# Output projection that ends with block 7, and a fixed order for the first tile pair of the MLP's up stage

## The chip, the cores and the metric

The kernel runs on one core of a Trainium2 chip. The metric is the device time of one execution in microseconds (us). Three runs of the kernel before gave 2959.98, 2953.46 and 2958.82 us; the median is 2958.82.

A core has five engines that each take their own instructions in order: PE (TensorE, matrix products; PEld is its weight load), DVE (VectorE), ACT (ScalarE), POOL (GpSimd) and SP (SyncE, which issues the DMAs here). They meet only through semaphores. PE writes PSUM, a small memory of eight banks of 128 x 512 float32; DVE and ACT read it from there. Everything else lies in SBUF.

## The reference

The reference is one streaming step of a two-layer network: layer 0 is a gated linear recurrence, layer 1 is differential attention, and each is followed by an output projection and a squared-ReLU MLP. Cut to what the change touches:

```
m = o @ w_o                                   # output projection, 1024 -> 1024
h = h + rmsnorm(m, norm_g[l, 1])
a = rmsnorm(h, norm_g[l, 2])
f = square(relu(a @ w_up)) @ w_down           # 1024 -> 4096 -> 1024
h = h + rmsnorm(f, norm_g[l, 3])
```

There are 1024 prompt rows and 128 sample rows; the kernel treats them as nine blocks of 128 rows, 0 to 7 for the prompt and 8 for the sample. All is float32.

## The kernel before

**Products.** A float32 operand is split into a high part (cast to the multiplier's format, on ACT) and a low part (the difference, on DVE). A product is then three matmuls: high x high, high x low, low x high.

**Output projection** (`out_proj`, lines 624 to 668). For each block, 48 matmuls (L281 to L283) into the tile `pm`; then the block's chain: a sum of squares on ACT (L216 on `pm`), a few tiny operations for the reciprocal root (L203 to L211), `t<-pm` on DVE (L655), `hb<-hb,t` (L658), a second sum of squares (L216 on `hb`), the tiny operations again, and `t<-hb` (L275), the normed row block. Halves of 512 columns of `t` are transposed on PE (`half_T`, four transposes into one bank: L242), and from PSUM ACT writes the high part (L246) and DVE the low part (L247) into the big operand tiles `aTh` and `aTl`. Blocks go in the order 0 to 8 in layer 0, and 0 4 1 5 2 6 3 7 8 in layer 1 (`LATE`), where one column half of blocks 0 to 3 was projected earlier (`EARLY`), so that 24 matmuls are left for each of these.

**Up stage** (`mlp_up`). The prompt part of `a @ w_up` is done by a seven-product scheme (Strassen-Winograd) on 2 x 2 quarters: rows of blocks 0 to 3 against rows of blocks 4 to 7, columns 0:512 against 512:1024. A11 and A12 are the two column halves of blocks 0 to 3, A22 the second half of blocks 4 to 7; S1 to S4 are sums of quarters. `pair_sums(blk, j)` forms them for blocks j and j+4 in place (L678 to L681, four operations of 128 x 512, on DVE or POOL). S2 goes to the aT tiles; S1, S3 and S4 are transposed by `s_ops` into the tiles a1, a3, a4 (high `h`, low `l`), one `half_T` per j, through two PSUM banks `T` (L235 for the transposes).

The 4096 columns are taken as 16 pairs of tiles. Per pair there are seven products P1 to P7 of 12 matmuls (L238, 128 x 512), and `smp`, the sample block against the same weights (24 matmuls of 128 x 256 into bank U). P1 and P2 use A11 and A12; P4 A22; P5 S1; P6 S2; P7 S3; P3 S4. The raw weights of a pair and their sums (`sums`, L735 to L738, on DVE for the first pair, then on POOL) are split as s0, s1, s2 in turn (L720 ACT, L721 DVE): s0 raw and s1 sums for the first pair, s2 raw and s0 sums for the second. Results are added up on DVE: c11 = P1 + P2 (L797), u2 = P6 + p1 (L823), c22 = P7 on top of P6, + p1 + P5 (L832, L833), c12 = P3 on top of P5, + u2 (L850), c21 = P4 on top of P7 and P6, + p1 (L865). PSUM bank tags are X, U, Y (two), Z (two), T (two).

The first pair goes in the order `P1 P2 T S1 P6 S3 P5 S4 P7 smp P3 P4`, where T is the split of s1. The two transposes of the sample block and the split of the second pair's weights stand with S4 and P7. `keep` holds the tiles `t`; the area of s2 is laid over it after S4.

**What sets the order.** The tile layer keeps each engine's list in an order that its own time model finds, under the data's dependencies; PE's up-stage matmuls are pinned in program order (`pin`, L228). ACT and DVE are not pinned.

Of the kernel before, what the change touches and what calls it, by code (L numbers as in the profile page):

```python
# [2 lines left out]

# [16 lines left out]
P = 128  # L20
D = 1024
# [34 lines left out]
SAMPLE = ['yk0 yl1 yn0', 'ys0', 'xf0', 'xk1 xn1 yv0', 'ys1', 'xf1', 'xl2 yv1', '']  # L56

EARLY = {1: (0,), 2: (1,), 6: (2,), 7: (3,)}
LATE = (0, 4, 1, 5, 2, 6, 3, 7, 8)
PAIR = 2  # L60


def view(ap, off, dims):
# [4 lines left out]
def tile_kernel(ctx, tc, x_prompt, x_sample, cache_k, cache_v, state_hgrn, norm_g, w_hgrn_in,  # L68
# [539 lines left out]
    def out_proj(w, gains, gain, o_src, osc, g_post, h_old, h_new, g_pre, order, W=None, early={}):  # L608
# [3 lines left out]
        with ExitStack() as os_:  # L612
# [9 lines left out]
                if b not in early:  # L622
                    prepare(block(b), b, o_src, osc, gain, pp, ts)

            order = LATE if early else range(NB)
            todo = [b for b in order if b not in early]
            for b in todo[:3]:
                prep(b)
# [4 lines left out]
            for b in order:  # L633
                pm = ps_wide("pm")
                halves = [early[b]] if early.get(b) is not None else []
                for nh in range(len(halves), 2):
                    halves.append(pm[:, nh * 512:(nh + 1) * 512])
                    out_half(halves[nh], W, nh, b)
                if todo:
                    prep(todo.pop(0))  # L640
                t = block(b) if b in early else blk[b]
                if early.get(b) is not None:
                    ss = ts.tile([P, 2], F32, name="ss", bufs=3)
                    for nh in range(2):
# [12 lines left out]
                nc.sync.dma_start(out=hb, in_=h_old(b))  # L657
                (nc.gpsimd if b in POOL_OUT else nc.vector).tensor_tensor(out=hb, in0=hb, in1=t, op=ALU.add)  # L658
                nc.sync.dma_start(out=h_new[b * P:(b + 1) * P, :], in_=hb)
                pre_norm(hb, g2, t, t, ts, b)  # L660
                done.add(b)
                if b == NBP:
                    continue
                if b < NP:
                    half_T(t[:, 0:512], aTh[:, b, 0:4], aTl[:, b, 0:4])
                half_T(t[:, 512:D], aTh[:, b, 4:8], aTl[:, b, 4:8])
                if b < NBP and b ^ NP in done:
                    pair_sums(blk, b % NP, nc.vector if len(done) > NBP - 3 else nc.gpsimd)
        return blk, keep

    def pair_sums(blk, j, eng):

        e, o = blk[j], blk[j + NP]
        a11, a12, a21, a22 = e[:, 0:512], e[:, 512:D], o[:, 0:512], o[:, 512:D]
# [2 lines left out]
        tt(out=a21, in0=a11, in1=a21, op=ALU.subtract)  # L679
        tt(out=a11, in0=a22, in1=a11, op=ALU.subtract)  # L680
        tt(out=a12, in0=a12, in1=a11, op=ALU.subtract)  # L681
        half_T(a11, aTh[:, j + NP, 0:4], aTl[:, j + NP, 0:4])

    def again(*a, **k):

# [2 lines left out]
    def mlp_up(l, blk, keep):  # L688
        wu = w_up[l].rearrange("(k p) n -> p k n", p=P)
        with ExitStack() as ms, ExitStack() as ls:  # L690
            R = Area(ms, "ur", "wst s0h s0l s1h s1l a4h a1h a1l a3h a3l a4l p1 u2 c0 hs", side="right")
            B = Area(ms, "ub", "X U Y:2 Z:2 T:2", space=PSUM)
            L = []
            SA = {}
            mk = {"A11": (0, 0), "A12": (0, 4), "S2": (NP, 0), "A22": (NP, 4)}
# [19 lines left out]
            def split(st, n, parts):

# [63 lines left out]
            for i in range(NFP):  # L780
                sets = (raw, tset)
                C = {}
                seq = "P1 P2 T S1 P6 S3 P5 S4 P7 smp P3 P4" if i == 0 else "P1 P6 P2 P5 P7 smp P3 P4"
                for op in seq.split():
                    if op == "P1":
                        X = bank("X")
# [5 lines left out]
                    elif op == "P2":  # L792
                        c = C["c11"] = cell()
                        if i == 0:
                            V = bank("Z")
                            prod(V, op, sets, True)
                            add(out=c, in0=V, in1=p1, op=ALU.add)  # L797
                            nc.scalar.activation(c, c, AF.Relu)
                        else:
                            prod(X, op, sets, False)  # L800
                            nc.scalar.activation(c, X, AF.Relu)
                        nc.gpsimd.tensor_tensor(out=c, in0=c, in1=c, op=ALU.mult)
                        store(c, "A11", i)
                    elif op == "T":
                        tset = split(st, 1, [(r1, ca), (r0, ca)])
                        sets = (raw, tset)
                        nx = load(1)
                    elif op == "S1":
                        s_ops(op, lambda j: blk[j + NP][:, 512:D])
                    elif op == "S3":  # L810
                        s_ops(op, lambda j: blk[j + NP][:, 0:512])
                    elif op == "S4":
                        s_ops(op, lambda j: blk[j][:, 512:D])
                        for z in range(2):
                            half_T(blk[NBP][:, z * 512:(z + 1) * 512], aTh[:, NBP, 4 * z:4 * z + 4],
                                   aTl[:, NBP, 4 * z:4 * z + 4], transpose, lambda n: bank("T"))
                        keep.close()
                        L.append(Area(ls, "ul", "s2h s2l c:7 hT"))
                    elif op == "P6":
                        Y = bank("Y")  # L820
                        prod(Y, op, sets, True)
# [6 lines left out]
                        prod(Z, op, sets, True)  # L828
                    elif op == "P7":
                        prod(Y, op, sets, False)  # L830
                        c = C["c22"] = cell()
                        add(out=c, in0=Y, in1=p1, op=ALU.add)  # L832
                        add(out=c, in0=c, in1=Z, op=ALU.add)  # L833
                        relu2(c)
                        store(c, "A22", i)
                        if nx is not None:
                            raw = split(nx, 2 * i + 2, [(r0, ca), (r1, ca)])
                            sums(nx, nc.gpsimd)
                    elif op == "smp":
# [7 lines left out]
                    elif op == "P3":  # L847
# [14 lines left out]
                    elif op == "P4":  # L862
# [695 lines left out]
```

## Time and profile before

| | us |
|---|---|
| runs | 2959.98, 2953.46, 2958.82 (median 2958.82) |
| profiled execution, its own time | 2951.5 |
| its span, first to last instruction | 2949.6 |
| PE busy in the span | 2856.6 (97%) |
| DVE / ACT / POOL busy | 1855.0 / 1205.4 / 669.3 |
| mean granted PE clock | 0.991 of full |
| layer 0: last block's projection ends, up stage begins | at 756.6 |
| layer 1: the same | at 2195.2 |

The span is measured from the first instruction to the last; the execution's own time is 1.9 us longer, and 7.3 us below the median of the three runs. "Busy" is the share in which an engine had an instruction under way. A timeline row has start, duration, engine, line, operation, output and inputs, shape and count; in brackets stands the idle time of that engine before it and what ended it. A row with x2 has two instructions merged.

### The profile page before, as it was taken

Reading aid. Unit: us, or ns where it says so; the run is one execution under the profiler, and the core shown is the slowest. Engines: PE = TensorE matmul, PEld = TensorE weight load, DVE = VectorE, ACT = ScalarE, POOL = GpSimd, SP = SyncE. Lnnn points to the kernel's source line nnn. Section 1 sums busy time; section 2 is a strip of 40 time slices with the busy share of each in tenths; the row PEclk is TensorE's granted clock in tenths of the full one; section 3 lists DMA queues with packets and bytes.
Section 4 is the critical chain, followed back from the end, with each engine's and each line's share of the span. In section 5 each row is a group of like instructions: output and inputs, shape, how many; then the busy total and the mean of one; then the engine's idle time right before and its main releaser. Section 6 shows DMA issues by size and latency. Waiting matters only on the chain. (4 is left out here: it accounts for less than half of the span.)

```text
span 2949.6 us, 45368 instructions
## 1 busy us (share of the span) xinstructions
PE 2856.6 (97%) x16897; PEld 2498.0 (85%) x16897; DVE 1855.0 (63%) x3523; ACT 1205.4 (41%) x2597; POOL 669.3 (23%) x558
## 2 busy tenths in 40 slices
PE   7999999989899999999989999998999999999998
PEld 6999999978688887888779999997877888878886
DVE  7777777776644445465875665656685444545567
ACT  5322222343333334443554554556543333434433
POOL 1111111101145442121211110111114454402311
PEclk9999999989999999999999999999999999999999
DMA  4111111142243348587752121313332433577966
GB/s 137 55 53 53 53 53 53 53 149 86 67 140 127 130 152 289 192 282 257 273 167 69 56 78 48 91 45 96 120 107 93 152 129 127 205 258 236 322 198 244
DMA packets 337120, 405.27 MB, mean 137 GB/s; under 512 B 21081, under 2 KB 210690, under 8 KB 336898
## 3 DMA queue, kind: packets, MB, share of 16 engines
q1 hardware_dynamic: 336898, 402.37, 41.3%
q8 instruction: 133, 2.18, 0.3%
q14 instruction: 89, 0.73, 0.1%
HBM read 280.12 MB, written 122.16 MB: 136 GB/s over the span
## 5 line engine op out<-in xcount | busy, mean ns | idle before, releaser
L238 PE MATMUL D<-wh,aTh 128*128 128x512 f32 x896 | 354.7, 396 | 2.8 <-DVE aO L1044 2.8
L238 PE MATMUL D<-wl,aTh 128*128 128x512 f32 x896 | 354.1, 395 | 0.5 <-DVE wl L905 0.5
L238 PE MATMUL D<-wh,aTl 128*128 128x512 f32 x896 | 354.2, 395 | 0.0
L905 DVE TENSOR_TENSOR aTl<-hst,aTh 128x1024 fp32r<-128x1024 f32 x112 | 156.2, 1399 | 186.2 <-ACT aTh L904 177.8
L238 PE MATMUL pj<-whi,aTh 128*128 128x256 f32 x864 | 254.2, 294 | 0.3
L238 PE MATMUL pj<-wlo,aTh 128*128 128x256 f32 x864 | 244.0, 282 | 2.3 <-DVE wlo L182 2.3
L238 PE MATMUL pj<-whi,aTl 128*128 128x256 f32 x864 | 244.1, 283 | 0.0
L904 ACT CAST aTh<-hst 128x1024 fp32r<-128x1024 f32 x112 | 116.7, 1048 | 247.8 <-PE D L238 217.3
L238 PEld LDWEIGHTS D<-wh,aTh 128*128 128x128 f32 x896 | 169.0, 189 | 43.7 <-issue 2.3
L238 PEld LDWEIGHTS D<-wl,aTh 128*128 128x128 f32 x896 | 169.1, 189 | 40.0 <-DVE wl L905 1.0
L238 PEld LDWEIGHTS D<-wh,aTl 128*128 128x128 f32 x896 | 169.1, 189 | 39.4
L238 PEld LDWEIGHTS pj<-whi,aTh 128*128 128x128 f32 x864 | 164.2, 190 | 6.6 <-issue 4.5
L281 PE MATMUL pi<-whi,aTh 128*128 128x256 f32 x576 | 167.1, 290 | 0.7 <-DVE qk L418 0.7
L238 PEld LDWEIGHTS pj<-wlo,aTh 128*128 128x128 f32 x864 | 163.9, 190 | 3.2 <-DVE wlo L182 2.5
L282 PE MATMUL pi<-wlo,aTh 128*128 128x256 f32 x576 | 166.5, 289 | 0.0
L283 PE MATMUL pi<-whi,aTl 128*128 128x256 f32 x576 | 166.3, 289 | 0.0
L238 PEld LDWEIGHTS pj<-whi,aTl 128*128 128x128 f32 x864 | 163.6, 189 | 0.0
L905 DVE TENSOR_TENSOR wl<-wsta,wh 128x1024 fp32r<-128x1024 f32 x112 | 138.9, 1244 | 22.7 <-ACT wh L904 21.2
L756 POOL TENSOR_TENSOR c<-c 128x512 f32<-128x512 f32 x96 | 115.0, 1198 | 166.0 <-ACT c L755 165.4
L755 ACT ACTIVATE c<-c 128x512 f32<-128x512 f32 x96 | 60.7, 632 | 223.1 <-DVE c L833 184.7
L904 ACT CAST wh<-wsta 128x1024 fp32r<-128x1024 f32 x112 | 117.1, 1049 | 77.9 <-PE D L238 28.3
L506 DVE COPY_PREDICATED A<-masks,lv 128x64 f32<-128x64 uint8 x448 | 85.7, 261 | 48.3 <-PE lv L503 44.3
(484 smaller groups left out, 7946.6 us busy)
## 6 DMA issues: line engine op xcount, KB each, us to landing
u_dr<-c SPq DMA_DIRECT2D x224, 256.0 KB, 4.3
hst<-u_dr SPq DMA_DIRECT2D x112, 512.0 KB, 5.4
wsta<-in_w_down_dram SPq DMA_DIRECT2D x96, 512.0 KB, 4.7
wst<-in_w_up_dram SPq DMA_DIRECT2D x32, 1024.0 KB, 6.1
wstb<-in_w_down_dram SPq DMA_DIRECT2D x32, 512.0 KB, 5.1
wstb<-t_dr SPq DMA_DIRECT2D x32, 512.0 KB, 5.3
h_dr<-hb SPq DMA_DIRECT2D x27, 512.0 KB, 2.6
hb<-h_dr SPq DMA_DIRECT2D x27, 512.0 KB, 4.6
```

Source lines behind the costliest of these rows:

```text
L238: pin(nc.tensor.matmul(*a, **k))
L281: matmul(out, lh, rh, start=first, stop=False)
L282: matmul(out, lh, rl, start=False, stop=False)
L283: matmul(out, ll, rh, start=False, stop=last)
L506: nc.vector.copy_predicated(out=view(A[:], o, [(per, 64 // m), (1, m)]), mask=masks[:, li, :].rearrange("p (j i) -> p j i", i=m), data=lv[ ...
L755: nc.scalar.activation(c, c, AF.Relu)
L756: nc.gpsimd.tensor_tensor(out=c, in0=c, in1=c, op=ALU.mult)
L904: nc.scalar.copy(h, st)
L905: vt(out=lo, in0=st, in1=h.bitcast(F32), op=ALU.subtract)
```

## The change

The block orders become 0 1 2 3 4 5 8 6 7 in layer 0 and 0 4 1 5 2 6 8 3 7 in layer 1. The last block (7) leaves the projection without being transposed; step A of the up stage does that, and its `pair_sums`. The first pair of the up stage follows a written list of steps, and inside it the PE, ACT and DVE instructions of the pair are chained in program order. The operands of S1 to S4 are made block by block between products; the sample's product comes after P1 and P2; P4 comes next and gets a bank of its own (Q, added to c21 by one more DVE operation); the second pair's weight split and sums (K) follow the last S4; c22, P3 and c21 end the pair. The order in which PSUM banks are laid out depends on the layer.

```
-LATE = (0, 4, 1, 5, 2, 6, 3, 7, 8)
+LATE = (0, 4, 1, 5, 2, 6, 8, 3, 7)
+FIRST_PAIR = "T P1 S1:01 P2 S1:2 N smp S3:0 A P4 S2:3 S1:3 C11 P6 S3:12 P5 S3:3 S4:0 P7 S4:123 K C22 P3 C21"
...
+    @contextmanager
+    def in_order():
+        traced = nc.cur_bb.bb.instructions
+        have = {id(i) for i in traced}
+        yield
+        for i in list(traced):
+            if id(i) not in have and i.engine in (mybir.EngineType.PE, mybir.EngineType.Activation,
+                                                  mybir.EngineType.DVE):
+                if i.engine in order_of:
+                    tc.add_manual_dep(i, order_of[i.engine].name, ..., reason="order")
+                order_of[i.engine] = i
...
-            order = LATE if early else range(NB)
+            order = LATE if early else (*range(6), NBP, 6, 7)
...
-                if b == NBP:
+                if b == NBP or len(done) == NB:
                     continue
...
-                    pair_sums(blk, b % NP, nc.vector if len(done) > NBP - 3 else nc.gpsimd)
+                    pair_sums(blk, b % NP, nc.vector if len(done) > NBP - 1 else nc.gpsimd)
...
-        half_T(a11, aTh[:, j + NP, 0:4], aTl[:, j + NP, 0:4])
+        if j < NP - 1:
+            half_T(a11, aTh[:, j + NP, 0:4], aTl[:, j + NP, 0:4])
...
-            B = Area(ms, "ub", "X U Y:2 Z:2 T:2", space=PSUM)
+            order = "X T_0 Y_0 Y_1 Z_0 T_1 Z_1 U" if l == 0 else "X T_0 Y_0 Y_1 Z_1 U Z_0 T_1"
+            B = Area(ms, "ub", order + " Y:2 Z:2 T:2", space=PSUM)
...
+            srcs = {"S1": (NP, 512), "S2": (0, 0), "S3": (NP, 0), "S4": (0, 512)}
+            def s_op(name, j):
+                n, (o, k) = name[1], srcs[name]
+                c = slice(j * P, (j + 1) * P)
+                if name == "S2":
+                    h, lo = aTh[:, NP + j, 0:4], aTl[:, NP + j, 0:4]
+                else:
...
+                    h, lo = [x[:, :, c] for x in SA[name]]
+                half_T(blk[o + j][:, k:k + 512], h, lo, transpose, lambda n: bank("T"))
...
-                seq = "P1 P2 T S1 P6 S3 P5 S4 P7 smp P3 P4" if i == 0 else "P1 P6 P2 P5 P7 smp P3 P4"
+                first = ExitStack()
+                if i == 0:
+                    first.enter_context(in_order())
+                seq = FIRST_PAIR if i == 0 else "P1 P6 P2 P5 P7 smp P3 P4"
...
+                    elif op[0] == "S":
+                        for j in op[3:]:
+                            s_op(op[:2], int(j))
+                    elif op == "A":
+                        b = NBP - 1
+                        half_T(blk[b][:, 512:D], aTh[:, b, 4:8], aTl[:, b, 4:8], transpose, lambda n: bank("T"))
+                        pair_sums(blk, b % NP, nc.vector)
+                    elif op == "N":
                         for z in range(2):
                             half_T(blk[NBP][:, z * 512:(z + 1) * 512], aTh[:, NBP, 4 * z:4 * z + 4],
                                    aTl[:, NBP, 4 * z:4 * z + 4], transpose, lambda n: bank("T"))
+                    elif op == "K":
                         keep.close()
                         L.append(Area(ls, "ul", "s2h s2l c:7 hT"))
+                        raw = split(nx, 2, [(r0, ca), (r1, ca)])
+                        sums(nx, nc.gpsimd)
+                    elif op == "P4" and i == 0:
+                        Q = bank("Y")
+                        prod(Q, op, sets, True)
...
+                    elif op == "C21":
+                        c = C["c21"] = cell()
+                        add(out=c, in0=Y, in1=p1, op=ALU.add)
+                        add(out=c, in0=c, in1=Q, op=ALU.add)
+                        relu2(c)
```

Lines move by about 19 to 50: a matmul of the up stage is L238 before and L257 now, a `half_T` evacuation L246/L247 before and L265/L266 now, the pair sums L678 to L681 are now L698 to L701, `t<-hb` L275 is now L294, the weight split L720/L721 is L749/L750.

VectorE, layer 0, the end of the first pair, before (s2 is the second pair's raw weights, s0 its sums; L832, L833 add up c22, L850 c12, L865 c21):

```order
L247 TENSOR_TENSOR a4l<-T,a4h 128x4x128 x2
L721 TENSOR_TENSOR s2l<-wst,s2h 128x1024 x2
L247 TENSOR_TENSOR a4l<-T,a4h 128x4x128 x2
L247 TENSOR_TENSOR aTl<-T,aTh 128x512 x2
L832 TENSOR_TENSOR c<-Y,p_8948 128x512
L833 TENSOR_TENSOR c<-c,Z 128x512
L850 TENSOR_TENSOR c<-Z,u_9019 128x512
L721 TENSOR_TENSOR s0l<-wst,s0h 128x1024 x2
L865 TENSOR_TENSOR c<-Y,p_8948 128x512
```

VectorE at the same place now (L877, L878 add up c22, L895 c12, L914, L915 c21):

```order
L266 TENSOR_TENSOR a4l<-T,a4h 128x4x128 x4
L750 TENSOR_TENSOR s2l<-wst,s2h 128x1024 x2
L877 TENSOR_TENSOR c<-Y,p_8938 128x512
L878 TENSOR_TENSOR c<-c,Z 128x512
L895 TENSOR_TENSOR c<-Z,u_9083 128x512
L750 TENSOR_TENSOR s0l<-wst,s0h 128x1024 x2
L914 TENSOR_TENSOR c<-Y,p_8938 128x512
L915 TENSOR_TENSOR c<-c,Y 128x512
```

The split of s2 stood between the second and the third a4; it now stands behind the fourth, directly ahead of the c22 additions.

VectorE, layer 0, where the last block's chain meets the first S1 operands, before:

```order
L203 TENSOR_SCALAR rs_v<-ss 128x1
L205 RECIPROCAL rs_y<-rs_y 128x1
L207 SCALAR_TENSOR_TENSOR rs_t<-rs_y,rs_v 128x1
L211 SCALAR_TENSOR_TENSOR rs_y<-rs_t,rs_y 128x1
L275 SCALAR_TENSOR_TENSOR t<-hb,rs_y,gb 128x1024
L797 TENSOR_TENSOR c_8950<-Z,p_8948 128x512
L247 TENSOR_TENSOR a1l<-T,a1h 128x4x128 x4
```

and now:

```order
L226 SCALAR_TENSOR_TENSOR rs_t<-rs_y,rs_v 128x1
L266 TENSOR_TENSOR aTl<-pt,aTh 128x512
L230 SCALAR_TENSOR_TENSOR rs_y<-rs_t,rs_y 128x1
L294 SCALAR_TENSOR_TENSOR t<-hb,rs_y,gb 128x1024
L266 TENSOR_TENSOR a1l<-T,a1h 128x4x128 x3
L266 TENSOR_TENSOR aTl<-T,aTh 128x512 x2
L266 TENSOR_TENSOR a3l<-T,a3h 128x4x128
```

The last block (8 before, 7 now) is normed directly ahead of the first a1 in both; c11 (L797) has moved behind the fourth a1.

PE, layer 1, the start of the up stage, before (`pm` is the last block's projection, X the bank of P1, `pt` the bank of a half_T in the projection):

```order
L281 MATMUL pm<-whi,aTh 128x512
L282 MATMUL pm<-wlo,aTh 128x512
L283 MATMUL pm<-whi,aTl 128x512
L238 MATMUL X<-aTh,s0h 128x512
L242 MATMUL pt<-ident,t 128x128 x4
L238 MATMUL X<-aTl,s0h 128x512
```

and now:

```order
L300 MATMUL pm<-whi,aTh 128x512
L301 MATMUL pm<-wlo,aTh 128x512
L302 MATMUL pm<-whi,aTl 128x512
L261 MATMUL pt<-ident,t 128x128 x8
L257 MATMUL X<-aTh,s0h 128x512
L257 MATMUL X<-aTl,s0h 128x512
```

The eight transposes ahead of X are the two halves of block 3, which is now the last but one; P1 reads the first of them and P2 the second.

## Rows read from the trace of the kernel before

**Rows 1.** Busy time of the engines in four stretches of the up stages (--windows).
Columns: stretch, its length, busy us and instructions of each engine, granted PE clock, DMA share, GB/s.

```profile
756.20:808.10 51.90, 39.50 (x194) 32.33 (x193) 33.17 (x51) 21.36 (x36) 11.34 (x10) 0.87 0.15 47
808.10:830.50 22.40, 22.40 (x111) 18.80 (x110) 10.67 (x13) 7.60 (x11) 11.08 (x10) 1.00 0.40 135
2195.20:2241.30 46.10, 37.30 (x192) 29.71 (x191) 31.48 (x49) 21.16 (x36) 11.16 (x9) 0.93 0.17 53
2241.30:2263.70 22.40, 22.40 (x111) 18.79 (x110) 10.67 (x13) 7.64 (x11) 11.09 (x10) 1.00 0.39 135
```

**Rows 2.** Waits of PE, layer 0, 640 to 860 us: total, times, longest.

```profile
PE pt L242 <- DVE t L680: 5.8, 1, 5.8
PE T L235 <- DVE a4l L247: 4.2, 2, 3.2
```

**Rows 3.** Waits of PE, layer 1, 2095 to 2310 us.

```profile
PE pt L242 <- DVE t L680: 4.7, 1, 4.7
```

**Rows 4.** Two idle stretches of PE, each with the stretch behind it (--windows).

```profile
760.40:766.20 5.80, 0.01 (x1) 0.03 (x1) 5.80 (x12) 1.73 (x3) 0.00 (x0) 0.89 0.00 0
766.20:771.40 5.20, 5.20 (x15) 4.22 (x16) 4.15 (x9) 1.94 (x4) 0.00 (x0) 0.50 0.90 299
787.50:790.80 3.30, 0.10 (x2) 0.06 (x1) 3.13 (x4) 1.39 (x3) 1.83 (x1) 0.70 0.00 0
790.80:795.50 4.70, 4.70 (x16) 4.02 (x16) 1.80 (x3) 1.17 (x2) 4.38 (x5) 0.50 0.00 0
```

**Rows 5.** Timeline of PE, layer 0.

```profile
756.58 0.40 PE L238 MATMUL X<-aTh,s0h 128*128 128x512 f32 x1
...
772.02 1.03 PE L235 MATMUL T<-ident,t 128*128 128x128 f32 x8
...
808.09 0.40 PE L238 MATMUL Y<-aTh,s0h 128*128 128x512 f32 x1
```

**Rows 6.** Timeline of PE, layer 1.

```profile
2195.21 0.39 PE L238 MATMUL X<-aTh,s0h 128*128 128x512 f32 x1
...
2241.28 0.40 PE L238 MATMUL Y<-aTh,s0h 128*128 128x512 f32 x1
```

**Rows 7.** Timeline of DVE, layer 0.

```profile
747.49 1.28 DVE L655 SCALAR_TENSOR_TENSOR t<-pm,rs_y,gb 128x1024 f32<-128x1024 f32 x1
748.81 1.23 DVE L658 TENSOR_TENSOR hb<-hb,t 128x1024 f32<-128x1024 f32 x1
...
773.27 0.69 DVE L247 TENSOR_TENSOR a1l<-T,a1h 128x512 fp32r<-128x512 f32 x1
...
787.66 2.36 DVE L721 TENSOR_TENSOR s2l<-wst,s2h 128x1024 fp32r<-128x1024 f32 x2 [0.81 <-ACT s2h L720]
...
797.01 0.69 DVE L832 TENSOR_TENSOR c<-Y,p 128x512 f32<-128x512 f32 x1 [2.95 <-PE Y L238]
797.74 0.69 DVE L833 TENSOR_TENSOR c<-c,Z 128x512 f32<-128x512 f32 x1
```

**Rows 8.** Timeline of ACT, layer 0.

```profile
745.20 1.02 ACT L216 ACTIVATE t<-pm 128x1024 f32<-128x1024 f32 x1 [2.39 <-issue]
...
772.65 0.58 ACT L246 CAST a1h<-T 128x512 fp32r<-128x512 f32 x1 [2.00 <-PE T L235]
...
785.91 2.01 ACT L720 CAST s2h<-wst 128x1024 fp32r<-128x1024 f32 x2
```

**Rows 9.** Timeline of POOL, layer 0: the second pair's weight sums.

```profile
788.97 2.18 POOL L735 TENSOR_TENSOR wst<-wst 128x512 f32<-128x512 f32 x1 [13.97 <-DVE s2l L721]
791.23 1.27 POOL L736 TENSOR_TENSOR wst<-wst 128x512 f32<-128x512 f32 x1
```

**Rows 10.** DMA issues, from the page: size, us from issue to landing.

```profile
h_dr<-hb SPq DMA_DIRECT2D x27, 512.0 KB, 2.6
```

**Rows 11.** Timeline of DVE, layer 1: one tiny operation at three times.

```profile
2147.59 0.89 DVE L207 SCALAR_TENSOR_TENSOR rs_t<-rs_y,rs_v 128x1 f32<-128x1 f32 x1
...
2148.59 1.26 DVE L207 SCALAR_TENSOR_TENSOR rs_t<-rs_y,rs_v 128x1 f32<-128x1 f32 x1
...
2208.38 0.22 DVE L207 SCALAR_TENSOR_TENSOR rs_t<-rs_y,rs_v 128x1 f32<-128x1 f32 x1
```

More of the change, by code (lines that the diff above doesn't have):

```diff
@@ L1 @@
 import math
-from contextlib import ExitStack
+from contextlib import ExitStack, contextmanager
 import concourse.bass as bass
@@ L195, in tile_kernel @@
     rsx = {}
+    order_of = {}
+    @contextmanager
[7 more added lines that the diff above has]
+                if i.engine in order_of:
+                    tc.add_manual_dep(i, order_of[i.engine].name,
+                                      mybir.DependencyInfo(mybir.DependencyClass.NoSync,
+                                                           mybir.DependencyReason.DATA), reason="order")
+                order_of[i.engine] = i
     def rstd_of(ss, n, inv_d, pool, y=None):
@@ L704, in a_op @@
                 return SA[name][0][:, k, :], SA[name][1][:, k, :]
-            def s_ops(name, src):
-                n = name[1]
-                SA[name] = h, lo = (R.tile([P, 4, HT], F32R, name=f"a{n}h", bufs=1),
+            srcs = {"S1": (NP, 512), "S2": (0, 0), "S3": (NP, 0), "S4": (0, 512)}
[5 more added lines that the diff above has]
+                else:
+                    if name not in SA:
+                        SA[name] = (R.tile([P, 4, HT], F32R, name=f"a{n}h", bufs=1),
                                     R.tile([P, 4, HT], F32R, name=f"a{n}l", bufs=1))
-                for j in range(NP):
-                    c = slice(j * P, (j + 1) * P)
-                    half_T(src(j), h[:, :, c], lo[:, :, c], transpose, lambda n: bank("T"))
+                    h, lo = [x[:, :, c] for x in SA[name]]
+                half_T(blk[o + j][:, k:k + 512], h, lo, transpose, lambda n: bank("T"))
             def split(st, n, parts):
@@ L796, in mlp_up @@
                             prod(V, op, sets, True)
[L797 to L801, printed above, removed]
+                            continue
+                        prod(X, op, sets, False)
+                        nc.scalar.activation(c, X, AF.Relu)
+                        nc.gpsimd.tensor_tensor(out=c, in0=c, in1=c, op=ALU.mult)
+                        store(c, "A11", i)
+                    elif op == "C11":
+                        c = C["c11"]
+                        add(out=c, in0=V, in1=p1, op=ALU.add)
+                        nc.scalar.activation(c, c, AF.Relu)
                         nc.gpsimd.tensor_tensor(out=c, in0=c, in1=c, op=ALU.mult)
@@ L807, in mlp_up @@
                         nx = load(1)
[L808 to L813, printed above, removed]
+                    elif op[0] == "S":
[6 more added lines that the diff above has]
+                    elif op == "N":
                         for z in range(2):
@@ L830, in mlp_up @@
                         prod(Y, op, sets, False)
+                    if op == "C22" or op == "P7" and i > 0:
                         c = C["c22"] = cell()
@@ L835, in mlp_up @@
                         store(c, "A22", i)
-                        if nx is not None:
+                        if nx is not None and i > 0:
                             raw = split(nx, 2 * i + 2, [(r0, ca), (r1, ca)])
                             sums(nx, nc.gpsimd)
-                    elif op == "smp":
+                    if op == "smp":
                         U = bank("U")
@@ L861, in mlp_up @@
                             tset = split(nx, 2 * i + 3, [(r1, ca), (r0, ca)])
-                    elif op == "P4":
+                    elif op == "P4" and i > 0:
                         prod(Y, op, sets, False)
@@ L866, in mlp_up @@
                         relu2(c)
+                    elif op == "C21":
[3 more added lines that the diff above has]
+                        relu2(c)
+                first.close()
                 pend = C
```

## Prediction

> **What bounds the kernel now.** I read first the busy times by stretch, then PE's waits, then the timelines around them. The first pair of each layer lasts 51.90 and 46.10 us with PE busy for 39.50 and 37.30; the pair behind it lasts 22.40 and PE is busy for all of it [rows 1]. So PE bounds the up stage from the second pair on, and whatever delays that pair's first dependent product, P6 (808.09 and 2241.28) [rows 5, 6], goes one to one to the end. In the first pair PE idles for 12.4 us (51.90 - 39.50) and 8.8 us. The waits that the trace names are `pt<-ident,t` on the pair sum of the last two blocks (5.8 and 4.7) and the T banks on a4l (4.2) [rows 2, 3]. The idle time is followed by work at 0.50 of full clock, that is 1.2 of 2.4 GHz: 5.2 us of it behind 5.8 us of idle, 4.7 us behind 3.3 [rows 4]. Half clock over 4.7 us costs some 2.35. A pair of 22.40 us is eight equal pieces (seven products and `smp`), 2.8 us each.
>
> The work to be done is nearly the same after: the same products and transposes, one more addition of 0.7 us on DVE per pair, and 0.7 us more on PE nowhere. What can change is only when the operands are ready. So I walked each engine's new list with the durations of before, 0.1 us for a handoff, and wrote down when PE waits.
>
> **Layer 0, the start.** X (P1) starts at about 756.2 instead of 756.58 [rows 5], since one half_T fewer stands ahead, and ends at 759.0; P2 ends at 762.9. The pair sums of blocks 2 and 6 are one chain with the last block's normalisation on DVE, and S1:2's transposes get their operand at about 764.7: 1.8 us idle. The 5.8 us wait of [rows 2] is gone here. But S1 takes only two T banks at first, and the next transpose waits until a1l(0) has read its bank. On DVE a1l(0) stands directly behind the last block's `t<-hb` (the second order listing), because a1 lies over `hb`; it also needs the store of `h_dr` to have landed (2.6 us [rows 10]). That `t<-hb` comes at 770.0 to 771.2, as the last chain goes at the same pace as before, so a1l(0) (0.69 [rows 7], behind a1h, 0.58 [rows 8]) ends at 771.9. PE idles 6.8 us and resumes at the moment at which S1's transposes started before (772.02 [rows 5]). Thus the pieces put ahead (P1, P2) were ahead before too, the wait has only another name, and `smp` (2.8 us), which used to fill a later gap, now stands behind this stall. Half clock follows for about 5 us as in [rows 4]; `smp` ends at 778.8.
>
> **Layer 0, the end of the first pair.** From there P4, P6, P5 and P7 (11.2 us) with six half_Ts of 0.52 (3.1; x8 is two of them in 1.03 [rows 5]) and 3.3 us of small waits for operands one half_T late bring P7's end to 796.4, S4's last transposes at 798.7. P3 is next, and it adds onto the Z bank that holds P5, so it waits until c22's second addition (L878) has read Z. In the first order listing that addition stands behind both s2l. The chain: a4h 0.58, the first s2h 1.0 (half of 2.01) [rows 8], two s2l 2.36, and two additions of 0.7 [rows 7] is 5.3, and with handoffs 5.65: P3 starts at 804.3. Before, L833 ran at 797.74, nine us behind the split of s2 (787.66) [rows 7], and `smp` covered it; here nothing covers it. What is queued behind it on DVE: c12, the split of s0, c21. Half clock then makes P3 5.1 us long (to 809.4). The second pair's P1 uses X and needs only s2 and runs to 812.4. Its P6 takes the bank of Q, which c21's second addition (L915) frees, and it needs s0, whose POOL sums start only once s2l is made (801.7) and take 6.4 by [rows 9] (2.18, 1.27, and two more of 1.27, with gaps) plus a square of 1.0 between: 809.2. Behind c12 (810.2) come its relu and hT on ACT (1.0), s0h (1.0), s0l (2.36) and two additions (1.4): 816.1. PE idles 3.7 us. That is 8.0 later than 808.09. 3.7 us of idle is nearest to the 3.3 of [rows 4], so I add 2.2 for half clock: **+10.2**.
>
> **Layer 1, the start.** Block 3 is now last but one, with only block 7's projection (48 matmuls, 4 x 2.8 = 11.2 us, ending at 2194.9) beside its chain, and X reads block 3. A chain's first half takes 4.84 us unimpeded, from its sum of squares at 745.20 to `hb` at 750.04 [rows 7, 8], and its second half the same 2.29 and 1.28 again: 8.4 us, so it would fit; but three s0h casts stand ahead of its second reciprocal root on ACT, four s0l (2.6 us) ahead of its `hb` on DVE, then the four weight sums (2.7). Walked so, `t<-hb` of block 3 ends at 2198.95, the eight transposes (third listing) wait for it 4.1 us, and aTl comes behind two s1l and block 7's `t<-pm`, at 2203.1. X starts effectively at 2202.9 instead of 2195.21 [rows 6], at half clock, and ends at 2207.85. P2 follows to 2211.4 (2209.5 before), and `smp` ends at 2216.75; here block 7's chain no longer stalls PE, so the 4.7 us of [rows 3] is absorbed in the earlier wait. From the end of `smp` everything goes as in layer 0, 37.3 us to P6: 2254.05, against 2241.28: 12.8 later, and 2.2 for the clock: **+15.0**.
>
> **The sum.** 10.2 + 15.0 = 25.2 on an execution of 2951.5: 2976.7. This execution lies 7.3 below the median, so 2984 on the median; I take 2980, between the two.
>
> **Terms not seen before.** (1) GpSimd beside DVE. Pair sums of blocks 2 and 6 in layer 1 go to POOL now, in the time of block 3's chain. While POOL did pair sums earlier, a tiny DVE operation took 0.89 and 1.26 instead of 0.22 [rows 11]: 1.7 us in all were lost over some 5.4 us of POOL's work. Of this about 1 is slack: +0.7 by the rows, at least 0; I leave it out of the sum. At most all 5.4 are lost, +4.4; this end is the rival (d) below. (2) The new bank order and the Q addition cost PE nothing: 0.7 us on DVE is in the chain above. (3) Half clock behind the 5.65 and 3.7 us: from 0 to 2.6 us each; I take the value nearest in [rows 4].
>
> Of (1) the Trainium skill, in "SBUF — State Buffer", section "SBUF: two separate sides", says that the port pair that GpSimd and VectorE share is an exclusive lock, held for a whole instruction, and that the other engine fully blocks. The two long rows agree in kind, yet DVE lost only 1.7 of 5.4 us; by the rule the sum would be nearer to +29 than to +25.
>
> **Rivals.**
> (a) The clock stays full behind the short stalls at P3 and P6. For it: the first stretch of [rows 1] has a mean clock of 0.87, so half clock is the smaller part of it; against it: both idle stretches of over 3 us in [rows 4] are followed by 0.50. P3 then ends at 807.15 and P6 comes at 814.0, +5.9 in layer 0 and +10.7 in layer 1: +16.6, 2968 to 2975.
> (b) The other side: c22's second addition is done before S4's last transposes end, because ACT and DVE run ahead of PE. For it: ACT is busy for only 21.36 of 51.90 us and DVE for 33.17 [rows 1]; against it: s2l stands behind the fourth a4l in DVE's list and cannot overtake it. From s2l done by 798.7, that is 5.65 us earlier, it decides: no stall at P3, none at P6 (s0 comes 5.6 earlier too), no half clock, 13.8 less per layer: 25.2 - 27.6 = -2.4, 2949 to 2956. It doesn't reach faster by 0.2%, save with a third of the starting stalls gone as well.
> (c) The last blocks' chains go at the unimpeded 8.4 us in both layers: layer 0's 6.8 us stall shrinks to about 1 and X in layer 1 isn't held. That leaves the two ends of the pair, and about +6.5: 2958 to 2966. Against it: before, with the same neighbours, the chain wasn't unimpeded.
> (d) DVE is blocked for the whole of POOL's pair sums, and the stores of `h_dr` land later than 2.6 us, so that a1l waits longer: +28 to +33, 2980 to 2992.
>
> **How the numbers follow.** Forecast 50%, with a range of its own of 2973 to 2987; (a) 20%, (d) 13%, (c) 8%, (b) 7%, and 2% for a gain that I don't see. About 0.2%, 5.9 us, is what a measurement can tell from no change. (b) lies within it or a little beyond, and most of (c) within it too: faster 0.06, same 0.10, slower 0.84. The range of 2960 to 2993 leaves out (b) and most that is beyond it on either side.
>
> **What would show it.** Right: in layer 0 a wait of T's transposes on a1l of about 7 us ending near 772; in both layers a wait of P3 (Z) on the c22 addition of 5 to 6 us, and of the second pair's P6 (Y) on c21 of 3 to 4, with 0.50 clock behind; P6 near 816 and, less layer 0's shift, near 2254; in layer 1 the transposes of `t` ahead of X wait 4 us; the pairs behind at 22.40. Wrong: P3 that follows S4's transposes without a wait (the end-of-pair terms fall, 8 us and more per layer), a first PE resumption in layer 0 well before 770, or X in layer 1 near 2196.

## The result, and the profile after

Four runs of the changed kernel gave 2980.68, 2981.65, 2983.99 and 2983.99 us: median 2982.82, against 2957.39 for the kernel before (four runs). The ratio is 1.0084 with a 95% interval of 1.0068 to 1.0100: slower by 25.4 us. The profiled execution spans 2979.0 us, 29.4 more than before.

Where the time went is seen first in three anchors: the first matmul of layer 0's down stage (into the bank D), the first matmul of its last group, and the first matmul of layer 1's down stage. Timeline of PE, before and then after:

```profile
1144.02 0.40 PE L238 MATMUL D<-wh,aTh 128*128 128x512 f32 x1
1494.76 0.47 PE L238 MATMUL D<-wh,aTh 128*128 128x512 f32 x1
2576.97 0.40 PE L238 MATMUL D<-wh,aTh 128*128 128x512 f32 x1
```

```profile
1157.05 0.40 PE L257 MATMUL D<-wh,aTh 128*128 128x512 f32 x1
1507.69 0.48 PE L257 MATMUL D<-wh,aTh 128*128 128x512 f32 x1
2607.39 0.40 PE L257 MATMUL D<-wh,aTh 128*128 128x512 f32 x1
```

Up to the down stage layer 0 lost 13.0 us; in that down stage nothing changed (350.74 and 350.64); from the second anchor to the third, with layer 1's attention, projection and up stage, 17.5 us were lost (1082.21 became 1099.70). With the 0.1 gained between them that makes 30.4; the last stretch gave 1.0 back.

The first pair and the second one of each layer, which answer to [rows 1] (stretch, length, busy us of PE, PEld, DVE, ACT, POOL, granted clock, DMA share, GB/s):

```profile
756.34:819.54 63.20, 40.16 (x196) 31.73 (x194) 35.93 (x55) 21.81 (x38) 9.97 (x9) 0.86 0.13 41
819.54:841.94 22.40, 22.40 (x103) 18.72 (x104) 11.07 (x13) 6.93 (x10) 11.19 (x9) 0.92 0.35 121
2208.70:2270.03 61.33, 42.68 (x195) 33.28 (x195) 34.26 (x55) 22.49 (x41) 9.65 (x8) 0.86 0.15 50
2270.03:2292.43 22.40, 22.39 (x103) 18.52 (x104) 11.57 (x13) 6.93 (x10) 11.08 (x9) 0.92 0.35 121
```

PE still has some 40 us of work in the first pair, but the pair lasts 63.2 us instead of 51.9 in layer 0 and 61.3 instead of 46.1 in layer 1. From the second pair on PE is busy all the time, so the delay of that pair's P6 (819.54 against 808.09, 11.5 us in layer 0) goes to the end, as before; the second pair's mean clock of 0.92, against 1.00 before, costs another 1.8 us (an estimate: 0.08 of 22.4 us).

The waits of PE in layer 0, which answer to [rows 2] (total, times, longest):

```profile
PE T L254 <- DVE a1l L266: 9.7, 2, 9.2
PE Z L257 <- DVE c L878: 5.4, 1, 5.4
PE Y L257 <- DVE c L915: 3.5, 1, 3.5
```

And in layer 1, which answer to [rows 3]:

```profile
PE Z L257 <- DVE c L878: 5.5, 1, 5.5
PE pt L261 <- DVE rs_y L230: 4.3, 1, 4.3
PE Y L257 <- DVE c L915: 3.4, 1, 3.4
PE X L257 <- DVE aTl L266: 1.5, 1, 1.5
PE T L254 <- DVE a1l L266: 1.0, 2, 0.8
```

Of the 5.8 us on a pair sum 1.4 are left, and the longest wait on a4l is gone. What has come: T on a1l, P3 (Z) on c22, the second pair's P6 (Y) on c21, and in layer 1 the transposes of block 3. The clock behind three of them, in layer 0, with the idle stretch ahead of each (as [rows 4]):

```profile
765.50:774.60 9.10, 0.00 (x0) 0.00 (x0) 5.49 (x11) 1.82 (x4) 0.00 (x0) 0.67 0.62 174
774.68:779.00 4.32, 3.77 (x17) 3.37 (x18) 1.89 (x4) 1.76 (x3) 0.00 (x0) 0.51 0.00 0
802.20:807.60 5.40, 0.00 (x0) 0.02 (x1) 4.34 (x5) 2.57 (x4) 2.43 (x2) 0.87 0.00 0
807.61:812.90 5.29, 5.29 (x13) 4.02 (x14) 0.00 (x0) 0.52 (x1) 4.53 (x4) 0.50 0.13 50
816.10:819.50 3.40, 0.00 (x0) 0.00 (x0) 3.25 (x4) 1.18 (x3) 0.00 (x0) 1.00 0.34 111
819.54:823.20 3.66, 3.66 (x9) 2.91 (x10) 1.96 (x3) 0.51 (x1) 1.04 (x1) 0.54 0.99 310
```

Behind each idle stretch the granted clock is 0.50 to 0.54, the lower level (1.2 of 2.4 GHz), over the 3.7 to 5.3 us shown.

The DVE rows of layer 0 that end the first two waits, which answer to [rows 7]:

```profile
770.01 1.28 DVE L294 SCALAR_TENSOR_TENSOR t<-hb,rs_y,gb 128x1024 f32<-128x1024 f32 x1
773.84 1.29 DVE L266 TENSOR_TENSOR a1l<-T,a1h 128x512 fp32r<-128x512 f32 x2 [2.54 <-DMA h_dr<-hb]
...
803.78 2.36 DVE L750 TENSOR_TENSOR s2l<-wst,s2h 128x1024 fp32r<-128x1024 f32 x2 [0.26 <-ACT s2h L749]
806.06 0.68 DVE L877 TENSOR_TENSOR c<-Y,p 128x512 f32<-128x512 f32 x1
806.78 0.69 DVE L878 TENSOR_TENSOR c<-c,Z 128x512 f32<-128x512 f32 x1
```

The second row is the one to read twice. The norm (L294) ended at 771.29, when the forecast had it (771.2), yet a1l came 2.54 us later: it waited for the store of `hb` to land. SP's rows show what stood ahead of that store:

```profile
765.94 0.38 SPq L758 DMA_DIRECT2D wst<-in_w_up_dram  x1
767.07 0.33 SPq L678 DMA_DIRECT2D h_dr<-hb  x1
```

The store of 512 KB was issued 1.1 us behind a load of 1024 KB, and a1l could start 6.8 us after its issue (773.84 - 767.07), where the median from issue to landing is 2.6 [rows 10]. In layer 1 the same pair stands 1.7 us apart (2216.44 and 2218.17), and DVE's row again waits for the store, until 7.4 us after its issue:

```profile
2225.60 1.29 DVE L266 TENSOR_TENSOR a1l<-T,a1h 128x512 fp32r<-128x512 f32 x2 [3.83 <-DMA h_dr<-hb]
```

In layer 1 of experiment 5 the load (2217.95) stands 3.7 us ahead of the store (2221.65), and a1l follows the norm at once, at 2225.34, so that this store needed at most 3.7 us. The load ahead is thus the likely reason; no run moved it alone.

The third wait, P6's on c21, hangs on the end of P3. c12 is added up when P3 is done (DVE, 813.11 to 813.80); ACT then does its relu and the copy of hT, and only then the split of s0. POOL had ended the weight sums at 812.21, earlier than c12 (in layer 1 2262.70 against 2264.30). Two rows of ACT and POOL's last sum:

```profile
813.84 0.63 ACT L784 ACTIVATE c<-c 128x512 f32<-128x512 f32 x1 [5.71 <-DVE c L895]
814.62 2.00 ACT L749 CAST s0h<-wst 128x1024 fp32r<-128x1024 f32 x2
```

```profile
810.93 1.28 POOL L767 TENSOR_TENSOR wst<-wst 128x512 f32<-128x512 f32 x1
```

### The profile page after: what moved, and what is told of

The parts are those of the page before. It is cut to its first block, busy times and chain, and to the rows that moved or that the text cites. A ratio compares the mean times of both kernels' runs of the same rounds, so it can differ in the third digit from the quotient of the medians.

```text
span 2979.0 us, 45363 instructions
## 1 busy us (share of the span) xinstructions
PE 2865.5 (96%) x16897; PEld 2503.4 (84%) x16897; DVE 1863.4 (63%) x3517; ACT 1206.5 (41%) x2597; POOL 681.9 (23%) x566
## 4 chain that ended last, share of the span: by engine, by line
PE 86%; DVE 6%; DMA 5%; ACT 2%; issue 1%; SPq 0%; POOL 0%; ACTq 0%; DVEq 0%; POOLq 0%
PE D L257 16%; PE pj L257 10%; PE Y L257 9%; PE Z L257 6%; PE X L257 5%; PE U L257 3%; PE S L257 3%; PE pi L300 2%; PE pi L301 2%; PE pi L302 2%; PE sc L257 2%; PE po L257 2%; PE pm L300 2%; PE pm L301 2%; PE pm L302 2%; DMA wsta<-in_w_down_dram 2%
## 5 line engine op out<-in xcount | busy, mean ns | idle before, releaser
L257 PE MATMUL D<-wh,aTh 128*128 128x512 f32 x896 | 354.3, 395 | 2.8 <-DVE aO L1095 2.8
L257 PE MATMUL D<-wh,aTl 128*128 128x512 f32 x896 | 353.5, 395 | 0.0
L257 PE MATMUL D<-wl,aTh 128*128 128x512 f32 x896 | 353.5, 395 | 0.0
L257 PE MATMUL pj<-whi,aTh 128*128 128x256 f32 x864 | 254.4, 294 | 0.3
L257 PE MATMUL pj<-wlo,aTh 128*128 128x256 f32 x864 | 244.1, 283 | 2.7 <-DVE wlo L184 2.7
L257 PE MATMUL pj<-whi,aTl 128*128 128x256 f32 x864 | 244.2, 283 | 0.0
L257 PEld LDWEIGHTS D<-wh,aTh 128*128 128x128 f32 x896 | 168.8, 188 | 43.6 <-issue 2.3
L257 PEld LDWEIGHTS D<-wh,aTl 128*128 128x128 f32 x896 | 168.8, 188 | 39.3
L257 PEld LDWEIGHTS D<-wl,aTh 128*128 128x128 f32 x896 | 168.8, 188 | 39.1 <-DVE wl L956 0.2
L257 PEld LDWEIGHTS pj<-whi,aTh 128*128 128x128 f32 x864 | 164.4, 190 | 6.5 <-issue 4.5
L257 PEld LDWEIGHTS pj<-wlo,aTh 128*128 128x128 f32 x864 | 164.1, 190 | 3.6 <-DVE wlo L184 2.9
L257 PEld LDWEIGHTS pj<-whi,aTl 128*128 128x128 f32 x864 | 163.8, 190 | 0.0
L1364 POOL COPY qq<-q 128x256 f32<-128x256 f32 x64 | 28.6, 447 | 390.5 <-PE pqT L254 259.9
```

Source lines behind the costliest of these rows:

```text
L257: pin(nc.tensor.matmul(*a, **k))
L1364: nc.gpsimd.tensor_copy(qq, view(Qb[h, i][:], (h % 2) * P, [(64, 2), (0, 2), (1, 64)]))
```

## The experiments

All times are medians; ratios are to the kernel before, run beside it on the same chip. Its median there was 2954.5 to 2957.8 us, so between experiments the ratios are the better measure. "The loss of a layer" is taken at the anchors above, from one profiled execution each; executions of one kernel lie up to 13 us apart (the kernel before, 23 runs), so 2 or 3 us in such a loss are not certain.

**1. c22 ahead of the split.** K is cut in two: the area is made, then c22, then the split and sums.

```diff
-... S4:0 P7 S4:123 K C22 P3 C21
+... S4:0 P7 S4:123 K C22 K2 P3 C21
```

> The two c22 additions are put ahead of the split of s2 (the area is set up before them as before). Theory: the waits of P3 and of the second pair's P6 hang on one chain (s2l, POOL's sums, s0, c21), so what is taken from the first is given back in the second with interest: P3's wait on c22 falls from 5.4 to about 3.0 us in each layer, s2l and POOL's sums come 1.4 us and more later, P6's wait on c21 grows from 3.4 to about 9, and P6 comes some 2.7 us later per layer: 2985 to 2990 us. Rival: each wait is worth its own size, so 2.4 us less per layer: about 2978.

Measured: 2986.16, ratio 1.0100 (1.0085 to 1.0115). PE's waits in layer 0:

```profile
PE Y L257 <- DVE c L916: 6.2, 1, 6.2
PE Z L257 <- DVE c L879: 2.8, 1, 2.8
```

P3's wait fell by 2.6 us and P6's grew by 2.7 (by 4.0 in layer 1, to 7.4). Two chains begin at the split of s2 and meet in s0: one by c22, P3 and c12, the other by POOL's sums. In the changed kernel the first ends last; here s2l came later and the second did, as ACT's wait ahead of s0h shows:

```profile
815.28 1.99 ACT L749 CAST s0h<-wst 128x1024 fp32r<-128x1024 f32 x2 [2.92 <-POOL wst L767]
```

Moving an addition from one to the other gains nothing. The size of P6's wait was less than expected (9), the time as expected.

**2. The split ahead of P7.**

```diff
-... S4:0 P7 S4:123 K C22 P3 C21
+... S4:0123 K P7 C22 P3 C21
```

> All four S4 blocks and then the split of s2 are put ahead of P7; nothing else. Theory: the split and POOL's sums start 2.5 to 3.3 us earlier, so P3's wait falls from 5.4 to about 2.9 us and P6, whose wait stays about 3.5, comes 2.5 to 3.3 earlier per layer: 2975 to 2978 us. Rival: c22 needs P7 and its two additions follow it at once, so what stands ahead of them matters little: 2981 to 2984.

Measured: 2974.01 (2969.91 to 2978.99), ratio 1.0060 (1.0045 to 1.0075): by the medians 8.8, by the ratios 7 us below the changed kernel. P3 waits 1.6 us in each layer instead of 5.4 and 5.5, P6 still 3.5. The loss up to layer 0's down stage fell from 13.0 to 7.5, that of layer 1 from 17.5 to 9.6. So what stands between P7 and c22 (the three S4 blocks and the split, moved together here) sets P3, not P7. Counted from the start of P1 the split came 2.3 us earlier. It was worth more than that, since P3 behind its shorter wait took 2.8 us instead of 5.3 at half clock; P6 follows the end of P3 by 6.6 us in both kernels.

**3. a1l and a4l trade places in SBUF.**

```diff
-"wst s0h s0l s1h s1l a4h a1h a1l a3h a3l a4l p1 u2 c0 hs"
+"wst s0h s0l s1h s1l a4h a1h a4l a3h a3l a1l p1 u2 c0 hs"
```

> The places of a1l and a4l in SBUF are swapped, so that a4l and not a1l lies where hb was; the first a1l then need neither the last block's norm nor its store. Theory: T's transposes wait for a1l only because of that place; the 9.2 us in layer 0 fall to 2 or 3 us, the sample's product runs in that time, and P6 comes 5 us earlier in layer 0 and 2 in layer 1: 2972 to 2976 us. Rival: only the store is in the way (2.5 us of idle DVE), the rest is block 7's chain, for which the half_T of A and P4 wait instead: 2979 to 2981.

Measured: 2982.65, ratio 1.0092 (1.0077 to 1.0107): no gain, against the theory's 2972 to 2976. But T's wait did fall to 2.2 us, and layer 0's first D stands at 1150.72, 6.3 us earlier than after. It was lost behind that: up to its last group layer 0's down stage took 4.1 us longer (354.8 against 350.6). PE's longest waits in that stage's first passes, here and in the changed kernel,

```profile
PE S L257 <- DVE aTl L956: 3.4, 1, 3.4
```

```profile
PE S L257 <- DVE aTl L956: 1.5, 2, 0.9
```

are on the low part of the sample's operand (`sst`, loaded back from the up stage's result). Here it came 9.1 us behind the first D, in the changed kernel 6.7. DVE's rows, here and there (`hst` is the prompt's operand):

```profile
1152.65 4.33 DVE L956 TENSOR_TENSOR aTl<-hst,aTh 128x1024 fp32r<-128x1024 f32 x3
...
1159.85 0.75 DVE L956 TENSOR_TENSOR aTl<-sst,aTh 128x256 fp32r<-128x256 f32 x2
```

```profile
1158.33 3.50 DVE L956 TENSOR_TENSOR aTl<-hst,aTh 128x1024 fp32r<-128x1024 f32 x3 [0.39 <-ACT aTh L955]
...
1163.73 0.41 DVE L956 TENSOR_TENSOR aTl<-sst,aTh 128x256 fp32r<-128x256 f32 x1
```

ACT had the high part at 1155.98 here, so the load was not late. The tile layer had put DVE's list in another order: a weight split stood ahead of the `hst` rows and L798 to L800 ahead of `sst`. The 5 us behind PE's wait went at a clock of 0.66. SP's loads had changed order too (those of `hb`, L1037, came 13 us ahead of the first D, in the changed kernel 3 us behind it); whether that cost anything is not shown.

**4. The same with a3l,** to tell the two apart.

```diff
-"... a4h a1h a1l a3h a3l a4l p1 u2 c0 hs"
+"... a4h a1h a3l a3h a1l a4l p1 u2 c0 hs"
```

> As the run with a1l and a4l swapped, but a3l takes the place of a1l, which is free two products earlier at the end of the up stage than a4l; the loads of the down stage should then keep their order. In the run with a4l, P6 came 6.3 us earlier in layer 0, but the first passes of the down stage waited for their operands 3 to 5 us longer per layer, and the whole was no faster. Theory: the gain is real and was lost to those loads, so here it stays: T's wait in layer 0 falls from 9.2 to about 2 us, the down stage begins with its old waits, 2974 to 2977 us. Rival: any earlier start is given back in the down stage: 2981 to 2984.

Measured: 2975.17, ratio 1.0070 (1.0057 to 1.0084); by the medians 7.6, by the ratios 4 us below the changed kernel. T waits 2.4 us in layer 0 instead of 9.7, D begins at 1151.18, the sample's low part comes 6.7 us behind it as in the changed kernel, and the down stage's wait is back at 1.5. So T's wait is the price of a1l's place over `hb`: norm and store together.

**5. Block 3 ahead of the sample in layer 1.**

```diff
-LATE = (0, 4, 1, 5, 2, 6, 8, 3, 7)
+LATE = (0, 4, 1, 5, 2, 6, 3, 8, 7)
```

> In layer 1 the order is 0 4 1 5 2 6 3 8 7: the sample stands between block 3 and block 7. Theory: the wait for block 3 ahead of X (4.3 and 1.5 us) goes, but block 7's chain, which sets the first a1l, ends as before, so T's transposes then wait 5 to 6 us instead of 1.0, as in layer 0: 2980 to 2983 us, nearly no gain. Rival: the hold of X was worth its 7.7 us: about 2975.

Measured: 2983.30, ratio 1.0086 (1.0069 to 1.0103). In layer 1:

```profile
PE T L254 <- DVE a1l L266: 5.2, 2, 4.7
```

Of the 4.3 and 1.5 us ahead of X 0.3 are left, P2 now waits 1.3, and T waits 5.2 instead of 1.0. The wait for block 3 covered a part of block 7's chain; removing it alone buys nothing.

**6. Without the chain on ACT and DVE.**

```diff
-                    first.enter_context(in_order())
+                    pass
```

> The chain that holds ACT and DVE to program order in the first pair is left out (PE's matmuls stay pinned). The tile layer then puts the split of s2 ahead of the third a4l in layer 0 and ahead of all a4l in layer 1. Theory: the fixed order is what puts c22 behind the split in layer 1, so P3's wait there falls from 5.5 to about 1 us and T's wait in layer 0 from 9.2 to 4 or 5; P3's wait in layer 0 stays: 2972 to 2977 us. Rival: PE's written order sets the waits and the other engines' lists don't matter: 2981 to 2984.

Measured: 2971.34 (to 2979.34), ratio 1.0065 (1.0049 to 1.0081). As expected P3 in layer 0 still waits (5.7), while in layer 1 it waits 1.1 on a4h and no longer on c22; T waits 2.6 us in layer 0, but the pair sum (4.3) and in layer 1 block 3's transposes (6.5, from 4.3) wait longer. The fixed order makes a part of the loss: 11 us by the medians, 6 by the ratios. By the anchors all of it is in layer 1 (8.1 us); of the 6.1 us gained in layer 0 up to its down stage 5.8 were lost within that stage.

**7 and 8. The two halves of the change apart.** First the block orders in the kernel before; then the new up stage with the old orders (sample last, block 7's transposes and pair sums back in the projection, no step A).

```diff
 # 7: kernel before
-LATE = (0, 4, 1, 5, 2, 6, 3, 7, 8)
+LATE = (0, 4, 1, 5, 2, 6, 8, 3, 7)
-order = LATE if early else range(NB)
+order = LATE if early else (*range(6), NBP, 6, 7)
 # 8: changed kernel, the reverse of 7, and
-... smp S3:0 A P4 S2:3 S1:3 C11 P6 ...
+... smp S3:0 P4 S1:3 C11 P6 ...
```

> The kernel before with the new block orders alone (0 1 2 3 4 5 8 6 7 and 0 4 1 5 2 6 8 3 7); its up stage is untouched, block 7 is transposed in the projection. Theory: the block order costs something by itself, since block 7's chain and, in layer 1, block 3's lie bare: in layer 1 PE waits 9 to 10 us ahead of X instead of 4.7; 2961 to 2966 us against 2957. Rival: the order of the blocks is free, and all of the loss lies in the up stage: 2955 to 2959.

> The changed up stage with the block orders of before (sample last): block 7's half_T and pair sums stand in the projection again, step A is gone; the rest of the written list is the same. With the kernel before (2957), the new blocks alone (2972) and both (2983) this is the fourth case. Theory: the up stage's list costs by itself what its waits at P3 (5.4) and P6 (3.4) cost with the half clock, 10 to 14 us in all, whatever the blocks: 2966 to 2972 us, so that the two parts add up (15 and 11 to 25). Rival: the up stage's list only loses with block 7 last: 2955 to 2960.

Measured: 2972.39, ratio 1.0059 (1.0045 to 1.0072), and 2976.62, ratio 1.0074 (1.0059 to 1.0089). Both expectations were too low. By the ratios the block orders cost 17 us alone, the up stage 22, both together 25: they overlap by some 14.

| loss, us | layer 0 to its down stage | layer 0's down stage | layer 1 to its down stage |
|---|---|---|---|
| new block orders (7) | 4.5 | 3.2 | 14.2 |
| new up stage (8) | 11.0 | 2.9 | 13.0 |
| both (the change) | 13.0 | -0.1 | 17.5 |

PE's longest wait of 7 in layer 1, and the longest ones of 8 there:

```profile
PE pt L242 <- DVE t L275: 9.1, 1, 9.1
```

```profile
PE Z L257 <- DVE c L877: 5.4, 1, 5.4
PE pt L261 <- DVE t L700: 4.4, 1, 4.4
PE Y L257 <- DVE c L914: 3.5, 1, 3.5
```

In 7 PE waits 9.1 us for block 3's norm, where the changed kernel waits 4.3 and 1.5 at that place; so part of what the block orders cost in the old list is not paid in the new one. In 8 the old wait on the last pair sums (4.7 in [rows 3]) is back, and P3 and P6 wait as in the changed kernel. Layer 0's down stage, which no edit touches, took 3 us more in 7 and 8. Near 1450 PE idles for about 3 us in all four kernels; behind it the granted clock from 1440 to 1480 stayed at 1.00 in the kernel before and the changed one, but was 0.91 for the first 20 us in 7, and 0.92 and 0.91 in 8. By an estimate from these (0.09 of 20 us, and 0.08 and 0.09 of it) that is 1.8 and 3.4 us. Why the clock fell in some profiled executions and not in others stays open.

**9 to 12. Putting the pieces together.** 9: the changes of 2, 4 and 5, the sample's product between P7 and c22, and in the second pair the sample's product ahead of P6 and P4 ahead of P3. 10: the old block orders with a rearranged list and the same second pair. 11: another list, and the first pair's weight sums on POOL. 12: 10 with the first pair's square of the sample's result on ACT.

```diff
 # 9 (with a1l and a3l swapped; block 3 ahead of the sample)
+T P1 S1:01 P2 S1:2 N S3:0 A P4 S2:3 S1:3 C11 P6 S3:12 P5 S3:3 S4:0123 K P7 smp C22 P3 C21
 # 10 (old orders, a1l and a3l swapped)
+T P1 S1:01 P2 S1:23 P6 S3:012 C11 P5 S3:3 S4:012 P4 S4:3 N K P7 smp C22 P3 C21
 # 11
+T P1 S1:01 P2 S1:2 P4 S2:3 S1:3 P6 S3:012 C11 P5 S3:3 S4:0123 N K P7 smp C22 P3 C21
-            sums(st, nc.vector)
+            sums(st, nc.gpsimd)
 # 9, 10, 11, 12: the second pair
-"P1 P6 P2 P5 P7 smp P3 P4"
+"P1 smp P6 P2 P5 P7 P4 P3" if i == 1 else "P1 P6 P2 P5 P7 smp P3 P4"
```

> The changed kernel with a1l and a3l swapped, block 3 ahead of the sample in layer 1, all of S4 and the split of s2 ahead of P7, the sample's product between P7 and c22, and in the second pair the sample's product ahead of P6 and P4 ahead of P3. Theory: the waits of P3 (5.4) and P6 (3.4) and most of T's (9.2) go in each layer, with the half clock behind them: some 12 us per layer, 2955 to 2962 us, level with the kernel before. Rival: the waits return elsewhere, as in the run with a4l: 2968 to 2975.

> Old block orders, the written list kept but rearranged: P6 right behind the S1 blocks, P4 between the S4 blocks, all S4 blocks and the split of s2 ahead of P7, the sample's transposes and product behind it; a1l and a3l swapped; in the second pair the sample's product ahead of P6 and P4 ahead of P3. Theory: of the waits of the changed kernel only the one on the last pair sums (about 5 us per layer, as before) is left, P3 and P6 wait for 0 to 1 us: 2948 to 2955 us against 2956. Rival: a fixed order loses against the tile layer's own in any form: 2960 and above.

> As the run with old blocks and a rearranged list, but P4 directly behind S1's third block, S2's last block in the up stage, and the first pair's weight sums on POOL instead of DVE. Theory: DVE has 2.7 us less ahead of the last pair sums, so PE's first wait falls from about 5 to 2 or 3 us in layer 0 and 4 in layer 1: 2946 to 2953 us. Rival: POOL's sums beside DVE slow DVE by what they take off it, so the wait stays near 5 and the time 2 to 5 us above the other run.

> As the run with old block orders and the rearranged list, but the first pair's square of the sample's result is done on ACT instead of POOL, where it stood behind three weight sums (PE waited 2.3 us for it in each layer). Theory: that wait goes, 2 to 2.5 us per layer: 4 to 5 us below that run's 2953.5, at 2948 to 2950, and faster than the kernel before by about 0.2%. Rival: the weight sums that follow set the next wait (s0 for the second pair's P6), so at most 1 us per layer: 2951 to 2954.

| | us | ratio (95%) |
|---|---|---|
| 9 | 2964.79 | 1.0035 (1.0022 to 1.0047) |
| 10 | 2953.48 | 0.9993 (0.9984 to 1.0001) |
| 11 | 2960.70 | 1.0019 (1.0010 to 1.0027) |
| 12 | 2954.34 | 0.9992 (0.9983 to 1.0001) |

9 took back 18 of 25 us by the medians and 14 by the ratios, less than expected: up to layer 0's down stage it loses only 1.3, in that stage 4.9 (clock 0.83 from 1440 to 1460), in layer 1 still 6.3, where T waits 3.2 us on a1l and X and P2 together 1.6 on aTl. 10 is level with the kernel before: P3 no longer waits, P6 only 0.4 and the second pair's P4 0.8, and the longest wait left is that on the last pair sums, 4.6 and 4.4 us. It keeps the new order of PSUM banks and the added operation for Q, so these two cost nothing that the measurement can tell. 11 is 7 us above 10 and differs from it in two things, the list and the place of the weight sums; its T waits 4.0 us on a1l where 10 waits 4.6 on the pair sum; which of the two costs was not tried. 12 was aimed at a wait of 2.3 us on `hs`, which I had put into the first pair. The wait stayed, and its row stands in the third pair:

```profile
842.94 0.44 PE L254 MATMUL U<-ident,hs 128*128 128x128 f32 x2 [2.33 <-POOL hs L893]
```

where the square, on POOL, stands behind weight sums:

```profile
841.05 1.26 POOL L766 TENSOR_TENSOR wst<-wst 128x512 f32<-128x512 f32 x1
842.28 0.61 POOL L893 TENSOR_TENSOR hs<-hs 128x256 f32<-128x256 f32 x1
```

The theory of 12 fell: a row in a list of waits tells how long the wait was, not where it stood. No version beats the kernel before by more than the measurement can tell.

## Why the prediction was right

- **The sum.** Forecast 2980, measured 2982.82. On the profiled execution 25.2 were forecast and 29.4 measured, 10.2 for layer 0 (13.0) and 15.0 for layer 1 (17.5). The waits were the forecast ones, in their places. That the medians differ by 25.4, so close to 25.2, is luck: on the profiles each layer lost 2.5 to 2.8 us more than forecast.
- **P3 on c22.** Forecast 5.65, measured 5.4 and 5.5, with the clock at 0.50 behind it: the chain a4h, s2h, s2l, two additions was as walked. Experiment 2 shows the cause. One reading was off, and nothing hangs on it: before, L833 ran 10.1 us behind the start of the split of s2, not nine.
- **The second pair's P6 on c21.** Forecast 3.7, measured 3.5 and 3.4, and by the path that the prediction walked: c12 (813.80) came later than POOL's sums (812.21), so the delay of P3 passes on to P6. Experiment 1 shows how near the other path is.
- **T on a1l in layer 0.** Forecast 6.8, measured 9.2, the term that was mis-sized most. The prediction took 2.6 us for the store from the median; this store held a1l until 6.8 us after its issue, so T resumed at 774.68 instead of 771.9. P3 (807.61 against 804.3) and P6 (819.54 against 816.1) are later by that 2.8 and some 0.6 more. The later landing stood in rival (d), and the 29.4 us of the profile lie within its 28 to 33; but its other half, DVE blocked for all of POOL's pair sums, did not come: while POOL did the sums of blocks 2 and 6 (2194.41 to 2200.70), the tiny operation took 1.16 us against 0.22 [rows 11], 0.9 us lost:

```profile
2199.56 1.16 DVE L226 SCALAR_TENSOR_TENSOR rs_t<-rs_y,rs_v 128x1 f32<-128x1 f32 x1
```

- **Layer 1's start.** The transposes of block 3 waited 4.3 (forecast 4.1), and X went on at half clock (0.50 from 2217.07 to 2221.90). Less the 12.9 us by which layer 0 ended later, X's second matmul came at 2204.1 (forecast 2202.9) and P6 at 2257.1 (2254.05). The 3 us more are not in one place: 1.2 at X, 0.8 from there to the end of `smp`, where T waited 1.0 on a1l, and 1.0 from `smp` to P6, as in layer 0. DVE's 3.8 us on the store cost PE only that 1.0, since X and P2 ran late themselves.
- **"X's hold is a loss of its own"** was not claimed but is easily read into the sum; experiment 5 shows that it isn't: without it T waits instead (5.2 us).
- **Rivals.** (a) The clock did not stay full: 0.50 and 0.54. (b) c22 was not done before S4's transposes: its second addition ended at 807.47, 5.3 us behind the last of them. (c) The chains were not unimpeded: block 7's first sum of squares (756.59) and its last `t` (770.01) lay 13.4 us apart, unimpeded 7.1.

## What to carry to other kernels

When an engine's order is written by hand, walk the other engines' lists to the point where the next stage's operands are made: here one weight split, placed behind the last operands of S4 and directly ahead of c22, held P3 and with it the next pair's P6, and was paid again in clock. When a second wait begins where the first one's work ends, shorten the chain that feeds the first; taking one step out of it may only let another chain end last. And look up which tile lies on which: here the place of a1l put it behind a norm and a store that nothing in the algorithm connects it with.

## What the runs showed that I had not expected

A store of 512 KB held its reader until 6.8 and 7.4 us after its issue when it was issued 1.1 and 1.7 us behind a load of 1024 KB; the median from issue to landing is 2.6, and 3.7 us behind such a load at most 3.7 were needed. And the place of one tile (experiments 3 and 4) changed the order of DVE's operations and of the loads in a stage some 370 us later: 6.3 us gained in one stage were gone by the end of the run. Last, the same idle time of some 3 us in layer 0's down stage was followed by half clock in some profiled executions and not in others (mean 0.91 to 1.00 over 20 us).
